# Moving the modulation's last weight tiles to other buffers and another queue, and splitting the last blocks of a retrieval

## The chip, the cores and the metric

The kernel runs on one core of a Trainium2 chip, as one program. The metric is the device time of one execution in microseconds. Three runs of the kernel before took 1963.52 us in the median (1961.88 to 1966.53).

## The reference

Two transformer blocks in float32 over 256 tokens of width 1024. The first mixes the tokens (pooling and a short convolution) and then retrieves experts: each of 8 heads picks, for each token, 16 of 16384 rows of `expert_u` and `expert_v`.

```python
u = expert_u[idx]
act = gelu(einsum('thkd,td->thk', u, hb))
out = einsum('thk,thkd->td', gates * act, expert_v[idx])
```

The second block is steered by one vector `c`:

```python
mod = silu(c) @ ada_w + ada_b          # 1024 -> 6 * 1024
sh1, sc1, gt1, sh2, sc2, gt2 = split(mod, 6)
h = rmsnorm(x, norm1_g) * (1 + sc1) + sh1
merged = sigmoid(ga)*(o_a @ w_branch_a) + sigmoid(gb)*(o_b @ w_branch_b) + sigmoid(gc)*(o_c @ w_branch_c)
x = x + gt1 * (merged @ w_out)
h2 = rmsnorm(x, norm2_g) * (1 + sc2) + sh2
x = x + gt2 * hier_moe(h2, ...)        # 32 experts of 1024 x 512, three matrices each
```

`o_a`, `o_b` and `o_c` come from an attention, a gated recurrence and a retention of four heads. Sections 2 to 5 of `mod` (`gt1`, `sh2`, `sc2`, `gt2`) are used only behind the three branches.

## The kernel before, in words

`phase_a` is the first block's mixer, `phase_b` its retrieval, `phase_c` the second block's three mixers and their branches, `phase_d` the output projection, the router and the 32 experts.

**Projections.** A weight tile is 128 partitions of 1024 floats (512 KB). `load_w` (L98 to L103) takes a buffer `wf` from a ring of four, issues the load from SyncE (L102), and `split` (L105) makes two parts of it: ScalarE casts the high part `wh` (L109), VectorE subtracts to get the low part `wl` (L110). `proj` then runs 24 matmuls with the tile: 16 with `wh` (L126), 8 with `wl` (L128); `proj_n` does the same with its operands swapped (L738). A `wf` buffer comes free when `wl` is written.

**Side work.** `Side` holds functions due at a tick; every projected tile is one tick (`E.side.tick()`).

**Modulation.** `modulation` computes `mod` without TensorE. Each of 48 steps takes a buffer, loads one tile of `ada_w` into it (L654, from SyncE), and two ticks later VectorE multiplies it by `silu(c)` and sums (L658, in place). Sixteen steps run in `phase_a`, with buffers of their own. The other 32 run in `phase_c`, one per tick, starting with branch b. There the buffer comes from the same ring of four as the weights: tag `wf`, `bufs=4`. In the stretch of those steps lie 8 tiles of branch b, 8 of the fourth retention head (`ret_head(3)`: 4 of `cv`, 4 of `cg`), 8 of the gates `gc` and 16 of branch c, 40 ticks in all.

**The mixers' buffers.** `phase_c` has a pool of `NBIG` = 27 buffers of 4 KB a partition, tag `t4`, through `c.t4` and `c.t8` (two buffers). When branch b starts, these hold the projections' input (4), `ob` (4), `merged` (2), both pairs of `oc` (8), the gates `gb` (2), and the rotated queries and keys of heads 2 and 3 (2): 22 of 27, and 2 more until retention head 2 has finished. Branch b frees 6, the last gate frees 4.

**Experts.** The experts' weights stream through a ring: the 27 `t4` buffers and spare buffers that other stages have done with. `Experts.load` (L1361) issues each load from SyncE as soon as its buffer is free; `used` asks for the next when TensorE has read a tile. Eight loads into `t4` buffers follow branch c (`ahead`), the others follow the output projection.

**Retrieval.** `phase_b` gathers one row pair per token and pick with an indirect transfer from GpSimd (L566) into one of 13 buffers `G`. Per pick VectorE makes the dot product with the token (L599), ScalarE the gelu (L603), VectorE multiplies by the gate into `gw` (L583), ScalarE puts `gw` on a diagonal `dg` (L575, four buffers), and TensorE adds the row, so weighted, to `acc` with 8 matmuls (L578). Gelu and gate are done for a block of picks at once: blocks of four, in the last head seven of four and four of one. Behind the last pick `x` takes `acc` (L615), is squared (L154), and `phase_c` begins.

The order of the instructions on each engine is fixed when the program is built, by a planner that goes by readiness on a model of the chip, with the program's order as priority; semaphores then hold the order.

Of the kernel before, what the change touches and what calls it, by code (L numbers as in the profile page):

```python
# [10 lines left out]
F32 = mybir.dt.float32  # L11
# [8 lines left out]
P = 128  # L20
# [225 lines left out]
def phase_a(E, x, mod, hm):  # L246


    nc, tc, d, side = E.nc, E.tc, E.d, E.side
    tt, ts, stt = nc.vector.tensor_tensor, nc.vector.tensor_scalar, nc.vector.scalar_tensor_tensor  # L250
    with tc.tile_pool(name="pa", bufs=1, reuse_waits="tile") as pa:
# [42 lines left out]

        final_squares(E, mod)
        c = pa.tile([P, 1024], F32, name="c_b")
        modulation(E, mod, c, lambda: pa.tile([P, 1024], F32, tag="aw", name=E.nm("aw"), bufs=3), range(16), 2.4)
        s = {}
        for pr in range(16):
            sec, o = divmod(2 * pr, 4)  # L300
# [227 lines left out]
def phase_b(E, x, M, hm):  # L528


    nc, tc, d, side = E.nc, E.tc, E.d, E.side
    tt = nc.vector.tensor_tensor
    with tc.tile_pool(name="pb", bufs=1, reuse_waits="tile", ) as pb:
# [30 lines left out]
        def gather(row):  # L564
            g = pb.tile([P, 2, D], F32, tag="G", name=E.nm("G"), bufs=NG)
            nc.gpsimd.indirect_dma_start(out=g.rearrange("p e d -> p (e d)"), out_offset=None, in_=d["expert_uv"],  # L566
                                         in_offset=bass.IndirectOffsetOnAxis(ap=row, axis=0))
            return g
# [12 lines left out]
        def gated(job):  # L581
            th, G, w, n, sc, gate = job
            tt(out=w, in0=sc, in1=gate, op=ALU.mult)  # L583
            values(job[:4])

        last = None
        for hd in range(8):
            todo = route.picks(s0, (1,), heads[0]) if hd == 0 else []
            share = [6, 5, 3, 3, 3, 3, 2, 2] if hd == 0 else [2] * 8
            if hd < 7:  # L590
                sc, steps = route.scores(hd + 1)
                todo += steps + route.picks(sc, (0, 1), heads[hd + 1], True)
            sizes = [4] * 8 if hd < 7 else [4] * 7 + [1] * 4
            for bi, n in enumerate(sizes):
                th, k0 = divmod(sum(sizes[:bi]), 16)
                G = [gather(heads[hd]["row", th][:, k0 + i:k0 + i + 1]) for i in range(n)]
                s, w = (pb.tile([P, GB], F32, tag=t, name=E.nm(t), bufs=4)[:, :n] for t in ("gs", "gw"))
                for i, g in enumerate(G):
                    nc.vector.scalar_tensor_tensor(out=g[:, 0, :], in0=g[:, 0, :], scalar=1.0, in1=hn[th], op0=ALU.mult, op1=ALU.mult,  # L599
                                                   accum_out=s[:, i:i + 1])  # L600
                    if i == min(1, n - 1) and last:
                        gated(last)
                nc.scalar.activation(s, s, AF.Gelu)  # L603
                last = (th, G, w, 16 * hd + k0, s, heads[hd]["gate", th][:, k0:k0 + n])
                if todo:
                    for f in todo[:share[bi]]:
                        f()
                    todo = todo[share[bi]:]
            for f in todo:
                f()  # L610
# [29 lines left out]
NWARM = 12  # L640


def modulation(E, mod, c, alloc, tiles, per):


    nc, d = E.nc, E.d

    def init():
        nc.sync.dma_start(c, d["c"])
        nc.scalar.activation(c, c, AF.Silu)  # L650

    def step(n):
        wt = alloc()
        nc.sync.dma_start(wt, d["ada_w"][n])  # L654
        E.side.at(2, lambda: total(n, wt))

    def total(n, wt):
        nc.vector.scalar_tensor_tensor(out=wt, in0=wt, scalar=1.0, in1=c, op0=ALU.mult, op1=ALU.mult, accum_out=mod[:, n:n + 1])  # L658
        if n % 8 == 7:
            section(n // 8)  # L660

    def section(sg):
        sl, a = slice(8 * sg, 8 * sg + 8), VEC["ada_b"][0] + 8 * sg
        nc.vector.tensor_tensor(out=mod[:, sl], in0=mod[:, sl], in1=E.vecs[:, a:a + 8], op=ALU.add)
        if sg in (1, 4):

            nc.vector.tensor_scalar(out=mod[:, sl], in0=mod[:, sl], scalar1=1.0, scalar2=None, op0=ALU.add)
            sg, names = (6, ("norm1_g", "g_final")) if sg == 1 else (8, ("norm2_g",))
            for nm in names:
                a = VEC[nm][0]  # L670
                nc.vector.tensor_tensor(out=mod[:, 8 * sg:8 * sg + 8], in0=mod[:, sl], in1=E.vecs[:, a:a + 8], op=ALU.mult)
                sl = slice(8 * sg, 8 * sg + 8)

    E.side.at(0, init)
    for i, n in enumerate(tiles):
        E.side.at(1 + int(i * per), lambda n=n: step(n))
# [9 lines left out]
def consts_c(E, pool):  # L686
    E.negmask = E.ctile("negmask", [P, 2, T], pool=pool)
    E.lvl = E.ctile("lvl", [P, 8, P], pool=pool)
# [17 lines left out]
def cat(t):  # L706
    return cols(t[0]) + cols(t[1])
# [332 lines left out]
def phase_c(E, x, mod, st):  # L1040

    nc, tc, d, side = E.nc, E.tc, E.d, E.side
    c = C()
    c.E = E
    c.sm = st.enter_context(tc.tile_pool(name="pcs", bufs=1, reuse_waits="tile"))
    c.big = st.enter_context(tc.tile_pool(name="pcb", bufs=NBIG, reuse_waits="tile"))
    sm = c.sm
    consts_c(E, sm)
    c.H = first_norms(E, c, x, mod)

    iq, ik = c.t4("iq", [P, 4, T]), sm.tile([P, 1, T], F32, name="ik", tag="ik")
    proj_to(E, c, "iq", 0, iq)
    proj_to(E, c, "ik", 0, ik)
    iw = index_weights(E, c)
    rel = sm.tile([P, 8, 3, P], F32, tag="s12", name="rel")
    nc.sync.dma_start(rel, d["rel_bias"])
    addm = dsa_select(E, c, iq, ik[:, 0, :], iw)
    aq, ak = c.t8("aq"), c.t8("ak")
    for n, a in (("aq", aq), ("ak", ak)):
        for i in range(2):  # L1060
            proj_to(E, c, n, 4 * i, a[i])
    side.at(1, lambda: end_first(E, x, aq[0][:, 0, 0:1]))
    av = [proj_n(E, c, "av", i) for i in (0, 1)]
    oa = (c.t8("oah", F32R), c.t8("oal", F32R))
    oa = (cat(oa[0]), cat(oa[1]))
    dsa_attend(E, c, cat(aq), cat(ak), av, rel, addm, oa)

    F, q, sg = c.t8("bf"), c.t8("bq"), c.t8("bg")
    v = []
    for i in range(2):  # L1070
        proj_to(E, c, "bf", 4 * i, F[i], AF.Sigmoid)
        proj_to(E, c, "bq", 4 * i, q[i])
        v.append(proj_n(E, c, "bi", i))
    for i in range(2):
        proj_to(E, c, "bg", 4 * i, sg[i], AF.Silu)
    side.drain()
    lb = lower_bound(E, c)
    ob = (c.t8("obh", F32R), c.t8("obl", F32R))
    n = 0
    for i in range(2):  # L1080
        for f in hgrn_half(E, c, lb, i, q[i], F[i], sg[i], v[i], ob[0][i], ob[1][i]):
            side.at(n, f)
            n += 1
        n += HG

    g = gates_(E, c, "ga")
    c.merged = c.t8("merged")
    branch(E, c, g, "w_branch_a", [oa], True)
    tab = c.t4("tab", [P, 2, T])
    nc.sync.dma_start(tab, d["rot"])  # L1090
    dec = sm.tile([P, 4, 3 * P], F32, name="dec", tag="s12")
    nc.sync.dma_start(dec, d["decay"])
    rot = []
    for i in range(2):
        for nm in ("cq", "ck"):
            xx, y = c.t4(nm, [P, 2, 2, T]), c.t4(nm + "r", [P, 2, 2, T])
            proj_to(E, c, nm, 4 * i, xx.rearrange("p h e t -> p (h e) t"))
            retention_rotate(E, c, tab, xx, y)
            rot.append(y)
    oc = []  # L1100

    def ret_head(h):
        if h % 2 == 0:
            oc.append((c.t8("och", F32R), c.t8("ocl", F32R)))
        vv = proj_n(E, c, "cv", h)
        gg = c.t4("csg", [P, 4, T])
        proj_to(E, c, "cg", 4 * h, gg, AF.Silu)
        retention_head(E, c, rot[2 * (h // 2)][:, h % 2], rot[2 * (h // 2) + 1][:, h % 2], vv, gg, dec[:, h, :],
                       oc[-1][0][h % 2], oc[-1][1][h % 2])

    ret_head(0)
    ret_head(1)
    g = gates_(E, c, "gb")
    ret_head(2)
    side.drain()
    modulation(E, mod, sm.tile([P, 1024], F32, name="c_b", tag="bA"),
               lambda: E.w.tile([P, 1024], F32, tag="wf", name=E.nm("aw"), bufs=4), range(16, 48), 1.0)
    branch(E, c, g, "w_branch_b", [(cat(ob[0]), cat(ob[1]))], False)
    ret_head(3)
    g = gates_(E, c, "gc")  # L1120

    c.ew, c.rows = Experts(E, c), sm.tile([P, 3, D], F32, tag="s12", name="rows")
    branch(E, c, g, "w_branch_c", [(cat(a), cat(b)) for a, b in oc], False)
    side.drain()
    ahead(E, c)
    return c
# [35 lines left out]
def first_norms(E, c, x, mod):  # L1162

    h = cat(c.t8("hb"))
    scaled(E, cols(x), E.col(48), h)
    H = (cat(c.t8("hbh", F32R)), cat(c.t8("hbl", F32R)))
    norm_split(E, h, E.r12, *H, sh=E.col(0))
    return H  # L1170
# [520 lines left out]
```

## Time and profile before

| | us |
|---|---|
| runs, median of 3 | 1963.52 |
| the profiled execution's own time | 1963.11 |
| its span | 1961.2 |
| PE busy | 1718.1 (88%) |
| DVE busy | 1099.2 (56%) |
| ACT busy | 581.8 (30%) |
| POOL busy | 384.2 (20%) |
| 630.31 MB moved, mean | 321 GB/s |

The span is the stretch from the first to the last instruction; the execution's own time is 1.9 us longer. In the page's slices the granted TensorE clock is 0.8 to 0.9 of full speed or more. The 16 DMA engines are full in the retrieval (about 200 to 850 us) and again from about 1480 us to the end, and half used between.

### The profile page before, as it was taken

The numbers are of one execution on the slowest core, as the hardware profiler recorded it, in microseconds if no ns is written. First come the engines' busy times: TensorE is split into PE (matmuls) and PEld (weight loads), VectorE is DVE, ScalarE is ACT, GpSimd is POOL, SyncE is SP. The second block draws the span as 40 slices with busy tenths as digits, with TensorE's granted clock in tenths as the row PEclk, the third lists the DMA queues.
The fourth block names the chain that finished last, engine by engine and source line by source line (L and its number), as shares of the span: only waits on it lengthen the run. The fifth ranks groups of instructions, "written<-read, shape, count | busy, mean of one in ns | idle before, by whom it ended". The sixth has DMA issues, their size and how long they took to land. (4 is left out here: it accounts for less than half of the span.)

```text
span 1961.2 us, 32932 instructions
## 1 busy us (share of the span) xinstructions
PE 1718.1 (88%) x13092; PEld 1424.8 (73%) x13092; DVE 1099.2 (56%) x2271; ACT 581.8 (30%) x1039; POOL 384.2 (20%) x294
## 2 busy tenths in 40 slices
PE   8999898878878787799999999998888978888886
PEld 8998898768877787789999999998786423322232
DVE  8868676686676766555766989777753000000001
ACT  5444231221221212134566253563442100000001
POOL 0001435545445454500000504100000000000000
PEclk8998999899999999989999999999989999999999
DMA  7853999999999999944545444357888999999998
GB/s 274 275 195 131 424 425 425 426 426 426 426 426 426 426 426 426 427 164 156 176 159 183 145 142 150 140 194 266 304 325 348 410 408 410 410 411 408 409 411 318
DMA packets 140994, 630.31 MB, mean 321 GB/s; under 512 B 16032, under 2 KB 16544, under 8 KB 107808
## 3 DMA queue, kind: packets, MB, share of 16 engines
q1 hardware_dynamic: 103968, 359.66, 49.2%
q0 software_dynamic: 36864, 268.45, 32.5%
q8 instruction: 106, 1.74, 0.3%
q14 instruction: 56, 0.46, 0.1%
HBM read 627.00 MB, written 1.05 MB: 320 GB/s over the span
## 5 line engine op out<-in xcount | busy, mean ns | idle before, releaser
L578 PE MATMUL sm<-dg,G 128*128 128x128 f32 x4096 | 502.6, 287 | 107.7 <-ACT dg L575 107.6
L578 PEld LDWEIGHTS sm<-dg,G 128*128 128x128 f32 x4096 | 492.7, 202 | 117.2 <-ACT dg L575 117.2
L566 POOL DMA_INDIRECT G<-expert_uv,row x256 | 316.1, 1235 | 516.4 <-DVE tf L481 192.7
L599 DVE SCALAR_TENSOR_TENSOR G<-G,hn 128x1024 f32<-128x1024 f32 x256 | 311.5, 1223 | 177.0 <-DMA G<-expert_uv,row 168.7
L110 DVE TENSOR_TENSOR wl<-wf,wh 128x1024 fp32r<-128x1024 f32 x237 | 300.4, 1270 | 147.7 <-ACT wh L109 135.1
L109 ACT CAST wh<-wf 128x1024 fp32r<-128x1024 f32 x237 | 248.5, 1049 | 382.1 <-PE mm L126 199.7
L1514 PE MATMUL mm<-ew,xg 128*32 128x512 f32 x836 | 199.4, 610 | 23.5 <-DMA ew<-e_up 9.3
L126 PE MATMUL mm<-hbh,wh 128*128 128x256 f32 x808 | 200.1, 289 | 8.5 <-ACT wh L109 4.9
L126 PE MATMUL mm<-hbl,wh 128*128 128x256 f32 x808 | 192.9, 280 | 0.0
L126 PEld LDWEIGHTS mm<-hbh,wh 128*128 128x128 f32 x808 | 153.1, 189 | 15.3 <-ACT wh L109 9.8
L1514 PEld LDWEIGHTS mm<-ew,xg 128*32 128x32 f32 x836 | 39.8, 110 | 159.1 <-DMA ew<-e_up 56.4
L126 PEld LDWEIGHTS mm<-hbl,wh 128*128 128x128 f32 x808 | 153.3, 190 | 0.8
L603 ACT ACTIVATE gs<-gs 128x4 f32<-128x4 f32 (+1 forms) x67 | 13.7, 205 | 417.1 <-DVE G L599 417.1
L128 PE MATMUL mm<-hbh,wl 128*128 128x256 f32 x808 | 109.8, 278 | 2.7 <-DVE wl L110 2.6
L128 PEld LDWEIGHTS mm<-hbh,wl 128*128 128x128 f32 x808 | 100.2, 188 | 3.5 <-DVE wl L110 3.5
L1548 PE MATMUL mm<-ew,s 128*32 128x256 f32 x896 | 81.1, 402 | 21.4 <-DMA ew<-e_down 20.6
L1519 DVE TENSOR_TENSOR s<-s,mm 128x512 f32<-128x512 f32 x8 | 5.5, 688 | 166.5 <-PE mm L1514 166.5
L575 ACT ACTIVATE dg<-ident,gw 128x128 f32<-128x128 f32 x256 | 84.1, 391 | 35.9 <-DVE gw L583 22.8
L1551 DVE TENSOR_TENSOR dn<-mm,rows 128x512 f32<-128x512 f32 (+1 forms) x18 | 11.4, 632 | 145.0 <-PE mm L1548 145.0
L126 PE MATMUL mm<-Hh,wh 128*128 128x256 f32 x400 | 90.0, 293 | 1.7 <-ACT Hh L753 1.6
L126 PE MATMUL mm<-Hl,wh 128*128 128x256 f32 x400 | 90.0, 290 | 0.4 <-DVE Hl L754 0.3
L1548 PEld LDWEIGHTS mm<-ew,s 128*32 128x32 f32 x896 | 34.3, 113 | 60.7 <-DMA ew<-e_down 38.7
(447 smaller groups left out, 2484.3 us busy)
## 6 DMA issues: line engine op xcount, KB each, us to landing
ew<-e_down SPq DMA_DIRECT2D x111, 512.0 KB
ew<-e_gate SPq DMA_DIRECT2D x109, 512.0 KB
wf<-w2t SPq DMA_DIRECT2D x101, 512.0 KB
ew<-e_up SPq DMA_DIRECT2D x100, 512.0 KB
aw<-ada_w SPq DMA_DIRECT2D x48, 512.0 KB
wf<-w_in SPq DMA_DIRECT2D x32, 512.0 KB
wf<-w2n SPq DMA_DIRECT2D x32, 512.0 KB
wf<-w_out SPq DMA_DIRECT2D x16, 512.0 KB
```

Source lines behind the costliest of these rows:

```text
L109: nc.scalar.copy(hi, src)
L110: nc.vector.tensor_tensor(out=lo, in0=src, in1=hi.bitcast(F32), op=ALU.subtract)
L126: mm(out, w[0][:, k * P:(k + 1) * P], x[e][k0 + k], start=first and k + e == 0, stop=False)
L128: mm(out, w[1][:, k * P:(k + 1) * P], x[0][k0 + k], start=False, stop=last and k == nk - 1)
L566: nc.gpsimd.indirect_dma_start(out=g.rearrange("p e d -> p (e d)"), out_offset=None, in_=d["expert_uv"], in_offset=bass.IndirectOffsetOnAx ...
L575: nc.scalar.activation(dg, E.ident, AF.Copy, scale=w[:, i:i + 1])
L578: nc.tensor.matmul(acc[k // 2][:, o:o + P], g[:, 1, k * P:(k + 1) * P], dg, start=n + i + th + k % 2 == 0, stop=n + i == 127, skip_group_c ...
L599: nc.vector.scalar_tensor_tensor(out=g[:, 0, :], in0=g[:, 0, :], scalar=1.0, in1=hn[th], op0=ALU.mult, op1=ALU.mult, accum_out=s[:, i:i + 1])
L603: nc.scalar.activation(s, s, AF.Gelu)
L1514: nc.tensor.matmul(gu[z][at(e), :], xg[k // 4][:, k % 4, at(e)], ew.up(p, name, k, e), start=k == 0, stop=k == KT - 1)
L1548: nc.tensor.matmul(ps[at(e), i:i + 256], hT[:, k, at(e)], ew.down(p, (a + i) // 256, k, e), start=i + k == 0, stop=k == 3, skip_group_chec ...
L1551: tt(out=dn[:, a:a + w], in0=ps[:, :w], in1=gt2[:, a:a + w], op=ALU.mult)
```

## The change

Two edits. `modulation` gets the queue and the distance in ticks between load and sum as arguments. `phase_a` passes what was there. `phase_c` passes GpSimd's queue, three ticks, and buffers of the mixers' pool. In the last head of the retrieval the sixth and seventh block of four become blocks of one: five blocks of four, then twelve of one.

```diff
-        modulation(E, mod, c, lambda: pa.tile([P, 1024], F32, tag="aw", name=E.nm("aw"), bufs=3), range(16), 2.4)
+        modulation(E, mod, c, lambda: pa.tile([P, 1024], F32, tag="aw", name=E.nm("aw"), bufs=3), range(16), 2.4, nc.sync, 2)
...
-            sizes = [4] * 8 if hd < 7 else [4] * 7 + [1] * 4
+            sizes = [4] * 8 if hd < 7 else [4] * 5 + [1] * 12
...
-def modulation(E, mod, c, alloc, tiles, per):
+def modulation(E, mod, c, alloc, tiles, per, queue, ahead):
...
     def step(n):
         wt = alloc()
-        nc.sync.dma_start(wt, d["ada_w"][n])
-        E.side.at(2, lambda: total(n, wt))
+        queue.dma_start(wt, d["ada_w"][n])
+        E.side.at(ahead, lambda: total(n, wt))
...
     modulation(E, mod, sm.tile([P, 1024], F32, name="c_b", tag="bA"),
-               lambda: E.w.tile([P, 1024], F32, tag="wf", name=E.nm("aw"), bufs=4), range(16, 48), 1.0)
+               lambda: c.t4("aw", [P, 1024]), range(16, 48), 1.0, nc.gpsimd, 3)
```

## Rows read from the trace of the kernel before

**Rows 1.** Chain that ended last, in order of time: start us, us, what.
```profile
1501.96 9.60 PE mm L1514 x65
1511.56 10.67 DMA ew<-e_gate
```

**Rows 2.** SyncE's queue in order of time: start us, us, what is issued.
```profile
1495.19 0.34 SPq L1361 DMA_DIRECT2D ew<-e_up  x1
1505.58 4.89 SPq L1361 DMA_DIRECT2D ew<-e_down  x8
```

**Rows 3.** Windows: stretch, length, busy of each engine, granted clock, DMA share, GB/s.
```profile
1180.00:1308.00 128.00, 124.50 (x1026) 122.01 (x1025) 109.60 (x114) 65.75 (x85) 30.09 (x13) 1.00 0.46 155
1308.00:1448.00 140.00, 124.74 (x999) 118.93 (x998) 103.91 (x140) 58.04 (x67) 0.00 (x0) 0.99 0.82 284
1448.00:1502.00 54.00, 42.14 (x342) 41.54 (x342) 28.30 (x83) 19.13 (x33) 0.00 (x0) 0.88 0.92 359
1502.00:1945.00 443.00, 381.33 (x2362) 129.06 (x2366) 25.42 (x47) 34.49 (x91) 0.00 (x0) 0.98 1.02 405
...
1500.00:1520.00 20.00, 18.04 (x143) 8.63 (x144) 2.63 (x6) 2.35 (x3) 0.00 (x0) 0.85 0.70 267
```

**Rows 4.** PE in order of time: the low-part matmuls that end two tiles.
```profile
1295.75 1.10 PE L128 MATMUL mm<-hbh,wl 128*128 128x256 f32 x8
...
1298.58 1.10 PE L128 MATMUL mm<-hbh,wl 128*128 128x256 f32 x8
```

**Rows 5.** Waits of PE, 1308 to 1448: in total, times, longest.
```profile
PE mm L126 <- ACT wh L109: 10.7, 14, 1.6
```

**Rows 6.** Waits of ACT, 1308 to 1448.
```profile
ACT wh L109 <- DMA wf<-w_branch_c: 20.7, 10, 3.6
```

**Rows 7.** Waits of SyncE's queue, 1308 to 1448.
```profile
SPq L102 <- DVE wl L110: 52.8, 29, 2.4
SPq L654 <- DVE aw L658: 23.5, 23, 2.9
```

**Rows 8.** SyncE's queue in order of time, two issues of the pattern.
```profile
1347.23 0.33 SPq L654 DMA_DIRECT2D aw<-ada_w  x1
1349.99 0.33 SPq L102 DMA_DIRECT2D wf<-w2t  x1
```

**Rows 9.** DVE by line, 1308 to 1448: busy, mean ns, idle before, releaser.
```profile
L658 DVE SCALAR_TENSOR_TENSOR aw<-aw,c_b 128x1024 f32<-128x1024 f32 x31 | 37.7, 1220 | 6.1 <-DMA aw<-ada_w 6.1
L782 DVE TENSOR_TENSOR s<-mm,gc 128x512 f32<-128x512 f32 x4 | 2.8, 692 | 6.1 <-PE mm L128 6.1
```

**Rows 10.** POOL in order of time: last gather, and the last work before the experts.
```profile
831.65 1.34 POOL L566 DMA_INDIRECT G<-expert_uv,row  x1 [1.10 <-DMA G<-expert_uv,row]
...
1242.66 2.97 POOL L921 TENSOR_TENSOR bkt<-bk,bQ 128x1024 f32<-128x1024 f32 x1 [4.70 <-PE sm L942]
```

**Rows 11.** PE in order of time, the retrieval's end.
```profile
823.38 7.41 PE L578 MATMUL sm<-dg,G 128*128 128x128 f32 x64 [0.94 <-ACT dg L575]
...
842.98 14.56 PE L578 MATMUL sm<-dg,G 128*128 128x128 f32 x128 [0.77 <-ACT dg L575]
```

**Rows 12.** DVE in order of time, the same end.
```profile
823.59 1.23 DVE L599 SCALAR_TENSOR_TENSOR G<-G,hn 128x1024 f32<-128x1024 f32 x1 [0.76 <-DMA G<-expert_uv,row]
...
850.60 1.23 DVE L599 SCALAR_TENSOR_TENSOR G<-G,hn 128x1024 f32<-128x1024 f32 x1 [0.80 <-DMA G<-expert_uv,row]
...
852.10 0.16 DVE L583 TENSOR_TENSOR gw<-gs,ex 128x1 f32<-128x1 f32 x1 [0.27 <-ACT gs L603]
856.24 2.48 DVE L615 TENSOR_TENSOR x<-sm,x 128x512 f32<-128x512 f32 x4 [3.98 <-PE sm L578]
```

**Rows 13.** ACT in order of time, the same end.
```profile
852.36 0.40 ACT L575 ACTIVATE dg<-ident,gw 128x128 f32<-128x128 f32 x1 [0.29 <-DVE gw L583]
...
854.07 0.29 ACT L175 ACTIVATE warm<-gw,eps 128x1 f32<-128x1 f32 x1
856.97 1.23 ACT L154 ACTIVATE sq<-x 128x512 f32<-128x512 f32 x2 [2.60 <-DVE x L615]
```

## The prediction, made before the changed kernel ran

> **What bounds the kernel now.** I began with the chain of waits, because the end is what a change must move. From 1511.56 us on it is a row of expert-weight transfers, with short pieces of TensorE between them; its first piece is TensorE's first use of expert tiles at 1501.96 [rows 1]. So two regimes meet at about 1502: behind it the transfers set the pace, before it something else decides when the experts start.
>
> What decides is seen in SyncE's queue. It issues an expert load at 1495.19 and then nothing until 1505.58 [rows 2]; the loads come from a ring of buffers, and the pause ends when TensorE's first products free some. The DMA share, 0.92 in the 54 us before, drops to 0.70 in 1500 to 1520 [rows 3]. The ring was full: what was left to load at 1502 is the total less the ring, whatever came before. The end is therefore the start of the experts plus a constant, 1961.2 - 1502.0 = 459.2 us, as long as the ring is full when they start.
>
> Then I followed TensorE backwards by windows. From 1180 to 1308 it is busy for 124.50 of 128 us; from 1308 to 1448, the stretch of the modulation's 32 tiles, for 124.74 of 140 us [rows 3]. A weight tile at full pace is 2.83 us (1295.75 to 1298.58) [rows 4], and in the second stretch TensorE waits for ScalarE's cast 14 times, 10.7 us together [rows 5], while ScalarE waits for branch c's weights alone 20.7 us to land, in ten waits [rows 6]. The weights land late since they are issued late: SyncE waits 52.8 us for `wl` and 23.5 us in front of the modulation's loads for the sums that free their buffers [rows 7], and the two kinds take turns [rows 8]. With four buffers shared, and one kind holding its buffer for two ticks, a weight is issued about one tile ahead.
>
> **The change, part by part.** The sum is made on the profiled execution, 1963.1 us (span 1961.2), 0.4 under the median of the runs.
>
> *Weights get the ring back.* The 32 loads leave the ring and SyncE's queue. TensorE's idle time is 140 - 124.7 = 15.3 us. Just before, with the same ring for weights alone, and VectorE at 109.6 of 128 us, it idles 3.5 of 128 [rows 3]. At that ratio the 124.7 us of work take 128.2: 11.8 us less. Bounds: nothing, if landings stay late; and at most all idle time, 15.3, plus what the modelled ends hide: eight matmuls are shown as 1.10 us [rows 4] though they start 2.83 / 24 = 0.118 apart, so that 0.16 us of each stall shows as busy; 14 stalls [rows 5] make 2.2, so 17.5. I take 11.8, the neighbour's row.
>
> *The loads on GpSimd.* GpSimd's last work in this stage ends at 1245.6 [rows 10], and the window shows 0.00 after it [rows 3]. What a plain load costs there no row shows. Nearest are SyncE's 0.33 us [rows 8] and the 1.34 us of a gather's issue [rows 10]; 32 loads in 140 us could each take 4.4, so either end costs nothing. I take the gather's. A load now waits for a `t4` buffer, of which 3 to 5 are free in branch b by the kernel's text; behind a waiting load stand only the later loads of the same kind, and who waits for them is VectorE's sum. With five in flight at the 1.29 us that 512 KB take at 405 GB/s [rows 3], shared by half with the weights, the last lands within 12.9 us; one buffer in five ticks is 14.2 us. It fits, without much to spare.
>
> *VectorE.* The sums stay, 1.22 us each [rows 9], a tick later in the program. VectorE is busy for 103.9 us [rows 3]; in 128 us that is 81%, and it does 86% in the stretch before, so it doesn't bind.
>
> *DMA engines.* They need 0.82 x 140 + 0.92 x 54 = 165 us of 194 now [rows 3], and would have 182. That is cover enough, and with the modulation off SyncE's queue the first expert loads can only move forward.
>
> *Singles in the retrieval.* The last gather is issued at 831.65 [rows 10] and its dot product starts at 850.60; the gate follows at 852.10 [rows 12], the diagonal ends at 852.36 + 0.40 = 852.76 [rows 13]. That is bandwidth, and stays. Today TensorE then still has work: it does the eight last picks in one piece from 842.98 to 857.54, 1.82 us each [rows 11], because picks 24 to 27 were released together. After the change picks 16 to 19 end at 830.79 as now [rows 11]; pick 20, with its dot product at 823.59 [rows 12], is ready 2.2 us later, and twelve picks at 1.85 could end by 853.0, before the last one is ready. So the last pick decides: 852.8 + 1.8 = 854.6, 2.9 us less. Eight more gelus, gates and diagonals lie beside gathers 2.45 us apart. What is late next is ScalarE: its table load and the small step behind it end at 854.36 [rows 13], while the squares now come 0.73 us behind the first update of `x` (856.97 against 856.24) and would be due at 854.1. 0.3 goes back, 2.6 us remain. Bounds: 0, if the planner orders it otherwise, and 2.9.
>
> Both gains lie before 1502 on the path that TensorE sets, so they add: 11.8 + 2.6 = 14.4 us, and 1963.1 - 14.4 = 1948.7, say 1949. With bounds of 0 to 17.5 and 0 to 2.9 the change, if nothing new comes late, lies between 1943 and 1963.
>
> **Rivals.** *The weights land as late as now, because the two streams meet in the engines.* For it: the DMA share is already 0.82, at only 284 GB/s [rows 3], and GpSimd, not held by ticks, can send several loads at once. Against it: the same engines move 405 GB/s later on [rows 3], and four buffers give a weight 8.5 us. Then only the retrieval's 2.6 us remain: 1960.5. The Trainium skill bears on this ("DMA: Bandwidth & Descriptors", section "Issuing engines are not separate DMA queues"): transfers from all queues run on the same 16 engines and interleave, so that another queue saves only the issue. By that rule alone the move of the queue is worth 32 x 0.33 = 10.6 us of SyncE's time, which is idle anyway, so nothing; what the rows show beside it is that SyncE's queue stands still in order, 23.5 us for other buffers, and that the rule doesn't count.
>
> *The expert ring isn't refilled in time.* If the loads between 1448 and 1502 (share 0.92) can't start sooner, only the hole goes: 0.30 of 20 us, 6 us, 1957. Against it: they wait for buffers that branch c frees, and branch c ends sooner.
>
> *Slower: VectorE stands in front of sums whose tiles have not landed.* Its queue is in order; behind a waiting sum stands the `wl` of the next weight, and behind that TensorE and the next load. Now five of 31 sums wait, 6.1 us, 1.22 each [rows 9]. If all 32 waited w, VectorE would need 103.9 + 6.1 (its waits for TensorE [rows 9]) + 32 w; that passes 140 + 2.6 from w = 1.0 on. With w = 1.22 the stretch takes 149, 9.0 more, and the time is 1963.1 + 9.0 - 2.6 = 1969.5. For it: the order on VectorE is planned on a model, and GpSimd's loads wait for scarce buffers. Against it: a tick more between load and sum, and nothing that stops GpSimd from running ahead. The Trainium skill has a rule that would bring it about ("SBUF — State Buffer", section "Who interferes with whom"): while VectorE runs an operation that takes the port pair it shares with GpSimd, GpSimd can't write the descriptors of its transfers. The operations that it names are copies, casts and tensor_scalar; here VectorE runs tensor_tensor and scalar_tensor_tensor, and beside scalar_tensor_tensor the last gather's issue took 1.34 us [rows 10]. I count it as a small part of this rival's chance.
>
> *The change doesn't do what it says*: no `t4` buffer is free when a load is planned, so the sums move back and branch c's end waits for `mod`. By the kernel's text there are 3 to 15; the price is that of the slower rival, and its chance is in it.
>
> **How the numbers follow.** Forecast 1949 with its own range of 1943 to 1956: 0.63. Late weights, 1956 to 1961.5: 0.15. Ring not refilled, about 1957: 0.08. Slower, 1967 and more: 0.13. Something else, 0.01. The time is that of the likeliest, 1949; 1941 to 1961 leaves out the slower case, a bit of the second and the far side of the first, 0.18. A measurement of this kernel tells 0.2%, 3.9 us, from no change. Faster by more: 0.63 + 0.08 + half of 0.15, so 0.78. Within: 0.09. Slower: 0.13.
>
> **What would show it.** Right: TensorE's waits for `wh` in the stretch of the 32 sums fall from 10.7 us to 3 or less and the stretch takes about 128 us; SyncE's queue has no waits for the modulation's sums; the last picks' matmuls end near 854.6; TensorE's first expert products come at about 1487.5, with SyncE again pausing just before, and 459 us lie behind them. Wrong: VectorE waits at the sums for `ada_w` tiles for more than a us each; weights still land late with GpSimd's loads in flight; no pause of SyncE before the first expert products; or more than 459 us behind them.

## The result, and the profile after

The changed kernel took 1936.7 us in the median of four runs (1935.37 to 1938.03), the one before 1963.1 in four runs beside it: a ratio of 0.9863 (95% interval 0.9846 to 0.988), 26.4 us less. 1949 was forecast, with a range of 1941 to 1961. The direction was right, the gain nearly twice the forecast one.

The profiled execution after has a span of 1933.1 us, 28.1 less. These points, all starts of matmuls read by their line, split it (us):

| | before | after | less in this piece |
|---|---|---|---|
| retrieval's last products (L578) | 857.3 | 854.7 | 2.6 |
| branch b's first low-part products (L128) | 1311.1 | 1307.1 | 1.4 |
| branch c's last low-part products (L128) | 1447.6 | 1427.9 | 15.7 |
| output projection's first low-part products (L128) | 1459.6 | 1432.8 | 7.1 |
| first expert products (L1514) | 1502.0 | 1473.9 | 1.3 |
| end of the span | 1961.2 | 1933.1 | 0.0 |

The windows of the kernel after, to be held against [rows 3] (stretch, length, busy time of PE, PEld, DVE, ACT, POOL, granted clock, DMA share, GB/s):

```profile
1176.00:1304.00 128.00, 124.50 (x1025) 122.00 (x1024) 108.42 (x112) 65.72 (x85) 32.83 (x18) 1.00 0.52 174
1304.00:1428.00 124.00, 119.96 (x996) 118.45 (x995) 105.14 (x148) 59.02 (x69) 14.24 (x27) 0.97 0.87 328
1428.00:1474.00 46.00, 40.27 (x345) 39.51 (x346) 26.00 (x77) 19.12 (x32) 0.00 (x0) 0.98 0.92 351
...
1472.00:1492.00 20.00, 18.12 (x143) 12.43 (x144) 2.63 (x6) 2.45 (x3) 0.00 (x0) 0.83 0.68 251
```

The stretch of the sums is 124 us where it was 140, with nearly the same number of products (996 against 999). Of TensorE's waits in it one is left, and it is not for a weight; it answers to [rows 5]:

```profile
PE sm L1023 <- DVE s L1022: 3.9, 1, 3.9
```

ScalarE, against [rows 6], now waits longest for TensorE, that is, it is ahead; branch c's weights are not in its list any more, though `w2t` still is:

```profile
ACT wh L109 <- PE mm L126: 30.1, 20, 2.5
ACT wh L109 <- DMA wf<-w2t: 14.6, 9, 3.3
```

SyncE's weight loads, against [rows 7], wait mostly for `wl`, which is the ring being full, and no longer for the sums at L658:

```profile
SPq L102 <- DVE wl L110: 82.5, 32, 7.1
```

GpSimd issues a load as a buffer of the pool comes free, from 1254.68 us on, long before the sums are due, of which the first starts at 1320.2. Later loads wait for sums to free their buffers, 15 of the 32, and no sum waits for them. The queue in order of time (start, length, idle time before and what ended it):

```profile
1254.68 0.59 POOL L654 DMA_DIRECT2D aw<-ada_w  x1 [13.08 <-PE sm L1002]
...
1367.74 1.67 POOL L654 DMA_DIRECT2D aw<-ada_w  x3 [9.27 <-DVE aw L658]
...
1383.18 0.53 POOL L654 DMA_DIRECT2D aw<-ada_w  x1 [1.88 <-PE mm L126]
```

At the retrieval's end TensorE, against [rows 11], does the last two picks one by one as they come, with small gaps (the trace holds 16 records a pick, two for each of its 8 matmuls):

```profile
850.48 2.05 PE L578 MATMUL sm<-dg,G 128*128 128x128 f32 x16 [0.25 <-ACT dg L575]
852.93 2.05 PE L578 MATMUL sm<-dg,G 128*128 128x128 f32 x16 [0.40 <-ACT dg L575]
855.09 3.89 PE L157 MATMUL mm<-sq,mod 128*128 128x256 f32 x16
```

The 7.1 us between branch c and the output projection were not in the forecast. In the kernel before, TensorE stands still between the two (PE in order of time):

```profile
1446.82 1.07 PE L128 MATMUL mm<-och,wl 128*128 128x256 f32 x8
1447.73 1.87 PE L1400 MATMUL mm<-router_w,mod 128*128 128x40 f32 x16
1456.06 0.58 PE L126 MATMUL mm<-mh,wh 128*128 128x256 f32 x1 [6.46 <-ACT wh L109]
1456.44 0.42 PE L126 MATMUL mm<-ml,wh 128*128 128x256 f32 x1
1456.66 0.41 PE L126 MATMUL mm<-mh,wh 128*128 128x256 f32 x1
1456.87 0.41 PE L126 MATMUL mm<-ml,wh 128*128 128x256 f32 x1
```

The cast that it waits for starts at 1454.96. Two things stand in front of it on ScalarE: in the planned order the last split of the merged branches (L753), which waits for VectorE, with a table load and a small step behind it; and, for the last 1.51 us, the projection's weights, which have not landed (kernel before, ScalarE):

```profile
1450.47 0.71 ACT L753 CAST mh<-merged 128x256 fp32r<-128x256 f32 x2 [6.00 <-DVE merged L783]
1451.20 1.28 ACT L175 ACT_TABLE_LOAD   x1
1453.16 0.29 ACT L175 ACTIVATE warm<-ml,eps 128x1 f32<-128x1 f32 x1 [0.67 <-DVE ml L754]
1454.96 1.04 ACT L109 CAST wh<-wf 128x1024 fp32r<-128x1024 f32 x1 [1.51 <-DMA wf<-w_out]
```

These weights were issued from SyncE behind eight expert loads (kernel before, SyncE's queue):

```profile
1436.47 6.60 SPq L1361 DMA_DIRECT2D ew<-e_gate  x8
1444.94 13.90 SPq L102 DMA_DIRECT2D wf<-w_out  x6
```

After, SyncE has sent four of the eight between branch c's weights, and the projection's loads go out eleven us before branch c ends:

```profile
1414.65 2.26 SPq L1361 DMA_DIRECT2D ew<-e_gate  x4
1417.00 12.34 SPq L102 DMA_DIRECT2D wf<-w_out  x5
```

So its first weights land while branch c still runs, and the planner has two of their casts in front of the last split (kernel after, ScalarE):

```profile
1426.68 1.05 ACT L109 CAST wh<-wf 128x1024 fp32r<-128x1024 f32 x1 [3.65 <-DMA wf<-w_out]
1427.91 1.04 ACT L109 CAST wh<-wf 128x1024 fp32r<-128x1024 f32 x1 [0.18 <-DMA wf<-w_out]
1430.79 0.71 ACT L753 CAST mh<-merged 128x256 fp32r<-128x256 f32 x2 [1.83 <-DVE merged L783]
```

TensorE goes on (kernel after, PE):

```profile
1427.26 0.96 PE L128 MATMUL mm<-och,wl 128*128 128x256 f32 x7
1428.05 1.87 PE L1400 MATMUL mm<-router_w,mod 128*128 128x40 f32 x16
1429.75 0.36 PE L126 MATMUL mm<-mh,wh 128*128 128x256 f32 x1
1429.95 0.28 PE L126 MATMUL mm<-ml,wh 128*128 128x256 f32 x1
1430.07 0.28 PE L126 MATMUL mm<-mh,wh 128*128 128x256 f32 x1
...
1432.29 0.39 PE L126 MATMUL mm<-ml,wh 128*128 128x256 f32 x1 [0.65 <-DVE ml L754]
```

SyncE again pauses before the first expert products, against [rows 2]:

```profile
1467.73 0.34 SPq L1361 DMA_DIRECT2D ew<-e_up  x1
1477.51 5.45 SPq L1361 DMA_DIRECT2D ew<-e_down  x8
```

### The profile page after: what moved, and what is told of

The parts are those of the page before. It is cut to its first block, busy times and chain, and to the rows that moved or that the text cites. A ratio compares the mean times of both kernels' runs of the same rounds, so it can differ in the third digit from the quotient of the medians.

```text
span 1933.1 us, 32931 instructions
## 1 busy us (share of the span) xinstructions
PE 1713.4 (89%) x13092; PEld 1428.9 (74%) x13092; DVE 1097.6 (57%) x2277; ACT 584.0 (30%) x1045; POOL 396.5 (21%) x326
## 5 line engine op out<-in xcount | busy, mean ns | idle before, releaser
L578 PE MATMUL sm<-dg,G 128*128 128x128 f32 x4096 | 506.9, 289 | 99.1 <-ACT dg L575 99.0
L578 PEld LDWEIGHTS sm<-dg,G 128*128 128x128 f32 x4096 | 497.3, 204 | 108.3 <-ACT dg L575 108.3
L566 POOL DMA_INDIRECT G<-expert_uv,row x256 | 310.9, 1215 | 521.7 <-DVE tf L481 191.5
L1514 PE MATMUL mm<-ew,xg 128*32 128x512 f32 x836 | 198.7, 613 | 22.2 <-DMA ew<-e_up 9.3
L1514 PEld LDWEIGHTS mm<-ew,xg 128*32 128x32 f32 x836 | 42.7, 110 | 154.3 <-DMA ew<-e_up 56.4
L128 PE MATMUL mm<-hbh,wl 128*128 128x256 f32 x808 | 110.9, 280 | 2.6 <-DVE wl L110 2.6
L128 PEld LDWEIGHTS mm<-hbh,wl 128*128 128x128 f32 x808 | 101.3, 190 | 3.4 <-DVE wl L110 3.4
```

Of the source, the lines that this page charges most:

```text
L128: mm(out, w[1][:, k * P:(k + 1) * P], x[0][k0 + k], start=False, stop=last and k == nk - 1)
L578: nc.tensor.matmul(acc[k // 2][:, o:o + P], g[:, 1, k * P:(k + 1) * P], dg, start=n + i + th + k % 2 == 0, stop=n + i == 127, skip_group_c ...
L1514: nc.tensor.matmul(gu[z][at(e), :], xg[k // 4][:, k % 4, at(e)], ew.up(p, name, k, e), start=k == 0, stop=k == KT - 1)
```

## The experiments

The points of every run, from its profile: the stretch from branch b's first to branch c's last low-part products, the gap from there to the projection's first, and what lies behind the first expert products. The ratio is to the kernel before on the same chip, with its interval.

| run | time, us | ratio | stretch | gap | behind |
|---|---|---|---|---|---|
| before | 1963.1 | | 136.5 | 12.0 | 459.2 |
| after | 1936.7 | 0.9863 (0.9846 to 0.988) | 120.8 | 4.9 | 459.2 |
| e1_picks | 1960.29 | 0.998 (0.9971 to 0.9989) | 135.2 | 11.3 | 461.0 |
| e2_mod | 1941.56 | 0.989 (0.9875 to 0.9905) | 119.3 | 4.9 | 460.2 |
| e3_buf | 1950.24 | 0.9937 (0.9922 to 0.9952) | 125.4 | 10.7 | 459.0 |
| e4_queue | 1971.71 | 1.0039 (1.0024 to 1.0055) | 151.1 | 4.9 | 458.9 |
| e5_npre0 | 1957.15 | 0.9966 (0.9954 to 0.9978) | 135.8 | 4.9 | 458.5 |
| e6_ahead2 | 1936.55 | 0.9862 (0.9837 to 0.9887) | 119.9 | 5.0 | 459.4 |
| e7_buf_npre0 | 1946.69 | 0.9908 (0.988 to 0.9937) | 127.2 | 4.9 | 458.8 |
| e8_spread | 1937.41 | 0.986 (0.9835 to 0.9886) | 117.4 | 7.5 | 459.3 |
| e9_ring19 | 1938.89 | 0.9873 (0.9856 to 0.9889) | 120.4 | 4.9 | 460.4 |
| e10_held8 | 1949.15 | 0.9937 (0.9914 to 0.996) | 121.0 | 7.9 | 468.0 |

**Each part alone.** e1_picks is the kernel before with one line changed, e2_mod the changed kernel with that line as it was:

```diff
-            sizes = [4] * 8 if hd < 7 else [4] * 7 + [1] * 4
+            sizes = [4] * 8 if hd < 7 else [4] * 5 + [1] * 12
```

> The kernel before with the last head's twelve single picks alone. Theory A (each part keeps its own share, and every us before the first expert product reaches the end): the last picks' matmuls end 2.6 us sooner and the time falls by 2.6 us, to about 1960.5; the stretch of the 32 sums stays at 140 us. Rival B (the singles also shift the planner's order and bring part of the 10 us that the sum did not foresee): a fall of 5 us or more.

> The modulation's part alone, with the old blocks of picks. Theory A: 26.4 - 2.6 = 23.8 us less than before, about 1939, with branch c's last product to the first of the output projection again about 5 us (12 in the kernel before). Rival B: clearly less than 21 us, since the two parts help each other.

The singles alone give 0.2% (2 to 6 us), the modulation alone 1.1% (19 to 25 us); the two make up the whole, and theory A holds in both. For e1_picks the times alone leave room for rival B's 5 us; its points do not, since stretch and gap together are 2.0 us shorter than in the kernel before, not 10. The 7.1 us at the gap come with the modulation.

**Buffers and queue apart.** From e2_mod, each with one of the two (e3_buf keeps the third tick as well):

```diff
 e3_buf
-               lambda: c.t4("aw", [P, 1024]), range(16, 48), 1.0, nc.gpsimd, 3)
+               lambda: c.t4("aw", [P, 1024]), range(16, 48), 1.0, nc.sync, 3)
 e4_queue
-               lambda: c.t4("aw", [P, 1024]), range(16, 48), 1.0, nc.gpsimd, 3)
+               lambda: E.w.tile([P, 1024], F32, tag="wf", name=E.nm("aw"), bufs=4), range(16, 48), 1.0, nc.gpsimd, 2)
```

> The modulation's tiles in the mixers' buffers, three ticks ahead, but still issued from SyncE; old blocks of picks. Theory A (the ring of four is what held the weights back; the queue is worth little): 15 us or more of the 23.8 come, about 1940 to 1948. Rival B (SyncE's queue in order is what held them: a weight's load stands behind a modulation load that waits for its buffer): under 8 us, 1955 or more.

> The modulation's tiles in the weights' ring of four as before, two ticks ahead, but issued from GpSimd; old blocks of picks. Theory A (the ring): no gain, 1960 to 1970, and ScalarE still waits for weights to land. Rival B (SyncE's queue): most of the 23.8 us come, 1945 or less.

Neither theory holds by itself. The buffers alone give 12.4 us (9 to 15), between the two expectations; the queue alone costs 7.7 us (5 to 11); together they give 21.6, so with the buffers there the queue is worth 9. In e3_buf SyncE still sends its loads in one order, six of the modulation's in a row before a weight of branch c, and eight expert loads before the projection's weights:

```profile
1382.70 3.45 SPq L654 DMA_DIRECT2D aw<-ada_w  x6
1386.24 1.29 SPq L102 DMA_DIRECT2D wf<-w_branch_c  x1
...
1423.44 6.95 SPq L1361 DMA_DIRECT2D ew<-e_gate  x8
1431.39 14.49 SPq L102 DMA_DIRECT2D wf<-w_out  x6
```

ScalarE waits for weights of branch c to land, once for 8.3 us (e3_buf, in total, times, longest):

```profile
ACT wh L109 <- DMA wf<-w_branch_c: 11.2, 3, 8.3
```

TensorE stands still behind either order, once in branch c and once at the gap (e3_buf, PE):

```profile
1398.99 0.39 PE L126 MATMUL mm<-och,wh 128*128 128x256 f32 x1 [3.94 <-ACT wh L109]
...
1443.09 0.58 PE L126 MATMUL mm<-mh,wh 128*128 128x256 f32 x1 [5.13 <-ACT wh L109]
```

In e4_queue both queues wait for buffers of the one ring. First VectorE's wait for the tiles, then SyncE's queue, which stands in front of weights until sums have freed buffers:

```profile
DVE aw L658 <- DMA aw<-ada_w: 23.2, 19, 3.5
```

```profile
SPq L102 <- DVE wl L110: 72.1, 26, 7.9
SPq L102 <- DVE aw L658: 36.8, 10, 6.4
```

19 sums wait 1.22 us each, the wait that the slower rival of the prediction asked of all 32, and in the shared ring, not in the pool. The stretch is 14.6 us longer where the rival had 9.0; how much of it VectorE's waits cost and how much SyncE's is not shown. The gap is 4.9 us all the same: here all eight expert loads go out between branch c's weights, from 1401.67 us on.

**The gap.** e5_npre0 is the kernel before, e7_buf_npre0 is e3_buf, both with

```diff
-NPRE, HG = 8, 2
+NPRE, HG = 0, 2
```

> The kernel before, with no expert loads between branch c and the output projection (NPRE 0 for 8); the same loads follow the projection's weights. Theory A (in the kernel before, eight expert loads stand in SyncE's queue ahead of the projection's first weights, and that made the 12.0 us between branch c's last and the projection's first low-part products): these become about 5 us, the time falls by 5 to 7 us, to 1956 to 1959. Rival B (the split of the merged branches, which waits 6.0 us for VectorE, sets the gap): it stays at 12 us and the time does not fall; or the expert ring fills later and the time grows.

> The modulation's tiles in the mixers' buffers from SyncE (e3_buf), with no expert loads between branch c and the output projection. Theory A: the gap goes from 10.7 to about 5 us and the time from 1950.2 to about 1944.5. Rival B: the gap stays, 1950.

The gap is 4.9 us in both, and the times fall by 6.7 us (4 to 9) against before and from a ratio of 0.9937 to 0.9908, whose intervals overlap. The weights of the projection now go out ahead of those expert loads (e5_npre0, SyncE's queue):

```profile
1437.30 0.43 SPq L1361 DMA_DIRECT2D ew<-e_down  x1
1438.61 5.54 SPq L102 DMA_DIRECT2D wf<-w_out  x3
1444.25 0.37 SPq L1361 DMA_DIRECT2D ew<-e_gate  x1
```

The last split of the merged branches still waits for VectorE there, but two of the projection's casts now stand in front of it on ScalarE (e5_npre0):

```profile
1446.92 1.05 ACT L109 CAST wh<-wf 128x1024 fp32r<-128x1024 f32 x1 [1.62 <-PE mm L126]
1449.64 1.05 ACT L109 CAST wh<-wf 128x1024 fp32r<-128x1024 f32 x1 [1.67 <-PE mm L126]
1453.09 0.71 ACT L753 CAST mh<-merged 128x256 fp32r<-128x256 f32 x2 [2.40 <-DVE merged L783]
```

So the eight expert loads in front of the projection's weights made the long gap, which is theory A. But the edit moved two things at once: the weights land earlier, and the planner, which goes by readiness, puts their casts before the split. The three kernels with a gap above 10 us (before, e1_picks, e3_buf) all have the casts behind the split, and there the weights themselves hold ScalarE up for only 1.51, 0.75 and 0.19 us. Rival B's split is thus part of the same gap. By these rows it took both: earlier weights alone, with ScalarE's order kept, would have saved little more than that, and an earlier place in the order alone nothing, as the weights had not landed. No run changes one without the other.

**The tick and the pace.** On the changed kernel:

```diff
 e6_ahead2
-               lambda: c.t4("aw", [P, 1024]), range(16, 48), 1.0, nc.gpsimd, 3)
+               lambda: c.t4("aw", [P, 1024]), range(16, 48), 1.0, nc.gpsimd, 2)
 e8_spread
-               lambda: c.t4("aw", [P, 1024]), range(16, 48), 1.0, nc.gpsimd, 3)
+               lambda: c.t4("aw", [P, 1024]), range(16, 48), 1.2, nc.gpsimd, 3)
```

> The changed kernel with two ticks instead of three between load and sum. Theory A (GpSimd's loads run ahead as buffers come free, so the tick doesn't matter): 1935 to 1939. Rival B (the third tick is what keeps VectorE from standing in front of tiles that have not landed): VectorE waits for ada_w tiles 10 us or more, and 1941 or more.

> The changed kernel with the 32 steps spread over 38 ticks instead of 32 (1.2 ticks each). Theory A (what idles TensorE in the stretch is VectorE, crowded by sums beside the retention head: one wait of 3.9 us): it goes, and 1933 come. Rival B (the last sums then stand in front of the merging of branch c and the projection): 1937 or more.

The third tick is worth nothing with the loads on GpSimd. Spreading the sums takes the wait at L1023 nearly away (0.6 us is left) and shortens the stretch by 3.4 us, and the gap grows by 2.6; nothing comes of it. Rival B named the sums for that, but no sum lies in the gap: the last one starts at 1414.71, 11.7 us before branch c's last products. ScalarE waits 4.92 us there for the projection's weights, which go out 8.1 us ahead of branch c's last products, 10.9 in the kernel after; what held them back is not shown. Theory A's wait went and its time did not come; rival B has the time and not the reason. Neither run beats the changed kernel.

**What lies behind the first expert products.** e9_ring19 shortens the list of the experts' ring:

```diff
-        self.got, self.ring = {}, [lambda: c.t4("ew", [P, 2, FF])] * NBIG
+        self.got, self.ring = {}, [lambda: c.t4("ew", [P, 2, FF])] * (NBIG - 8)
...
-    ew.load(NPRE, NBIG)
+    ew.load(NPRE, NBIG - 8)
```

> The changed kernel with eight buffers fewer in the experts' ring (19 of the mixers' 27, and the spare ones), the pool itself unchanged. Theory A (the ring is full when the experts start, and what lies behind is the rest of the weights at the engines' rate): TensorE's first expert products stay at about 1474 us in the profile, 8 x 512 KB at 404 GB/s, 10.4 us, are added behind them (459.2 becomes about 469.5), and the time is about 1947. Rival B (the stretch behind is set otherwise, or the ring isn't full when the experts start): it stays within 2 us of 459 and the time within 3 us of 1936.7.

460.4 us lie behind, so theory A seems to fall; but SyncE issues 14 loads in a row from 1471.16 us, while the first expert products come at 1480.4 in this run:

```profile
1469.46 0.80 SPq L1361 DMA_DIRECT2D ewx<-e_up  x2
1471.16 17.67 SPq L1361 DMA_DIRECT2D ew<-e_down  x14
```

The entries of the list are calls for any buffer of the pool, and the pool still had 27. The run tested nothing of the claim. e10_held8 takes the buffers themselves:

```diff
+    held = [c.t4("held", [P, 1024]) for _ in range(8)]
+    for t in held:
+        nc.vector.tensor_copy(t[:, 0:1], cat(c.merged)[7][:, 0:1])
...
         nc.vector.reciprocal(rs[th], rs[th])
+        if th:
+            for t in held:
+                tt(out=t[:, 0:1], in0=t[:, 0:1], in1=rs[1], op=ALU.mult)
```

> The changed kernel with eight of the mixers' 27 buffers kept from the experts: eight tiles are allocated at the end of branch c, written in one column, and read in the last step. (A shorter list of the ring, e9_ring19, did not do that: its loads still took every free buffer of the pool, as its queue shows from 1471 us on, before the first expert products.) Theory A (the buffers full at the experts' start set what is left to load): 8 x 512 KB at 404 GB/s, 10.4 us, come on top of the 459.2 us behind the first expert products, about 469.5 us, and the time is about 1947. Rival B (the stretch behind is set otherwise): it stays within 3 us of 459.2 and the time within 4 us of 1936.7.

The first expert products come at 1477.2, and 468.0 us lie behind them, 8.8 more for 10.4 expected; the time is 1949.15. The other 3.3 us of the profile lie ahead of the start, 3.0 of them at the gap, where all of VectorE's part of the split comes behind the writes into the eight buffers. Of the `e_up` tiles 4 are issued before the start, 12 in the kernel after: eight fewer. The DMA engines stand half idle before the start, as they must with less to fill, at 0.49 in 1460 to 1480 (columns as above; 0.67 in the kernel after):

```profile
1460.00:1480.00 20.00, 15.36 (x128) 13.71 (x130) 9.83 (x49) 6.80 (x14) 0.00 (x0) 0.96 0.49 183
```

Theory A holds. The eight buffers are gone for the whole of the experts' stage, so a slower stream could be a rival; but over 1474 to 1917 us the engines move 403 GB/s, against 404 in the kernel after. By this run a buffer that is full at the start is worth about 1.1 us (8.8 / 8); that a 28th would give as much is an estimate from it, which no run tests.

## Why the prediction was wrong

*Two regimes that meet at the experts' start: right.* 459.2 us lie behind the first expert products before and after, and 458.5 to 461.0 in all runs with the whole pool, whose starts lie between 1473.9 and 1511.3 us. Every us gained ahead of it reached the end.

*Singles: right, the exact size in part by luck.* 2.6 us were forecast for the path, and TensorE's first products behind the retrieval start 2.6 sooner (862.33 against 864.90 us). But the last picks end at 854.98, 0.4 later than forecast, and the 0.3 that ScalarE was to take back is not seen. The last products start at 853.7 to 855.8 us in the six kernels with the singles and at 856.6 to 858.9 in the six without.

*The step that failed: the stage between branch c and the experts was taken as fixed, its change at nothing, and it was worth 7.1 us.* I wrote that "with the modulation off SyncE's queue the first expert loads can only move forward". That was right, and I did not follow it to what stood behind these loads. The signs were in the trace before: 42.14 us busy of 54 in the window after branch c [rows 3]. e5_npre0 shows the cause without any of the change: take the expert loads from in front of the projection's weights, and 12.0 us are 4.9. Of the 7.1, 5.8 are the idle time itself (6.46 against 0.65); behind the long pause the first products start 0.21 us apart, where 0.12 is the pace of the kernel after. This term put the time outside the range: with 15.7 us for the stretch, 2.6 for the singles and nothing here the sum gives 1944.8, which lies inside.

*"Weights get the ring back", 11.8 us: the mechanism was right, the term too small.* The stretch became 15.7 us shorter, inside the term's bounds of 0 to 17.5; the four kernels with the same edit there (after, e2_mod, e9_ring19, e10_held8) have 15.5 to 17.2. I took TensorE's idle time from the column of the matmuls, 15.3 us, and let what the modelled ends hide, 0.16 us for each of 14 stalls, count in the upper bound only. The column beside it, of the weight loads, comes nearer: before, 118.93 of 140 us, idle for 21.1; in the stretch ahead, 122.01 of 128 [rows 3]. At that ratio 118.93 us of loads take 124.8, 15.2 less; after, they are busy for 118.45 of 124. The Trainium skill calls matmul busy time a bad metric and weight-load busy time a good one for how close a kernel is to its roofline, since matmuls are pipelined ("Trainium Kernel Development and Optimization", section "Performance Expectations"); of stalls it does not speak. Here the one column gives 11.8, the other 15.2, and 15.7 were measured; that is one pair of stretches, read after the fact.

The term also took ring and queue together. e3_buf, with the ring given back and SyncE's queue kept, gains 11.1 us in the stretch, and e2_mod, with both, 17.2: by these points the queue is worth about 6 in the stretch and 5.8 at the gap (the two spans differ by 10.8, the medians by 9).

*The queue, weighed by a rule.* By the Trainium skill's rule that the prediction cites ("DMA: Bandwidth & Descriptors", section "Issuing engines are not separate DMA queues") a second queue saves only the issue, and nothing was to be had. The prediction noted that the rule leaves out the order in a queue, and gave it no term of its own. With free buffers parting the two orders was worth 9 us, by e3_buf and e2_mod; without them, in e4_queue, the second queue cost 7.7. The measurement decides.

*The loads on GpSimd: right.* An issue takes 0.53 us, between the bounds of 0.33 and 1.34, and hides.

*Rivals.* Weights as late as now did not happen (one wait of TensorE is left). The ring was refilled in time, with SyncE's pause. VectorE did not stand in front of sums: no wait for an `ada_w` tile lies in the stretch. In e4_queue it did, with the other buffers.

*The remaining 2.7 us* of the profile's difference lie between the retrieval and branch b (1.4) and behind the projection's start (1.3). From the retrieval's end to branch b the twelve kernels have 452.4 to 456.0 us with the same work, and from the projection's first low-part products to the experts' start 41.1 to 43.7; 1.4 and 1.3 are within that spread, and neither has been followed further.

## What to carry to other kernels

Read TensorE's stalls from the weight-load column too, and compare with a stretch of the same work that is not disturbed; here that column came nearer. When a class of loads leaves an in-order queue, follow all that stood behind it, to the next stage's first load: here the gain at the hand-over was nearly half of that in the stage. Where a planner fixes the order, look also at what it moves when a load comes earlier. And ask of a buffer and a queue separately and together: here one alone gave a little over half, the other alone a loss.

## What the runs showed of the hardware that was not expected

After the 6.46 us pause TensorE's granted clock was 0.50 over 1456 to 1461 in the kernel before, the lower of its two levels (1.2 GHz), with products 0.21 us apart in place of 0.12; it was 0.79 over 1440 to 1460 as a whole. In the kernel after, over 1420 to 1440 with a pause of 0.65, it was 1.00. The one wait left in the stretch of the sums, 3.9 us at L1023, was followed by the same: 0.50 over 1370 to 1375, and products 0.21 apart. Each of these two pauses cost more than its length.

A plain load of 512 KB, issued from GpSimd, took 0.53 us of GpSimd's time, less than half of the gather's 1.34.
